# A copy of the SwiGLU gate by ScalarE between exponential and logarithm, in the filler of the recurrences

## The chip, the cores and the metric

The kernel runs on one core of one Trainium2 chip. The metric is the device time of the whole program in microseconds (us). The kernel before was timed three times on its own; beside these times there is one profiled execution, whose trace gives the start, the length and the waits of each instruction. TensorE is called PE in the rows, VectorE DVE, ScalarE ACT, GpSimd POOL, and SyncE, which issues the DMA transfers, SP.

## The reference, cut to what matters

The program is a trunk of two layers over one sequence of 1024 tokens with 1024 channels, all in fp32. Layer 0 mixes by forgetting attention and causal pooling, layer 1 by RWKV-7. Behind each mixer stands a SwiGLU feed-forward network (FFN) with 2816 inner columns, which are 22 blocks of 128:

```
def _swiglu(h, w_gate, w_up, w_down):
    return (jax.nn.silu(h @ w_gate) * (h @ w_up)) @ w_down

def _rwkv7_step(state, inp):
    r_t, w_t, k_t, v_t, a_t, b_t = inp
    sa = jnp.einsum('bhvk,bhk->bhv', state, a_t)
    state = (state * w_t[:, :, None, :] + sa[..., None] * b_t[:, :, None, :]
             + v_t[..., None] * k_t[:, :, None, :])
    return state, jnp.einsum('bhvk,bhk->bhv', state, r_t)
```

Here silu(z) is z times sigmoid(z). The change concerns how that product is formed in a part of the FFN blocks.

## The kernel before, in words

**Layout and products.** Channels lie on the 128 partitions, tokens on the free axis, in two halves of 512 tokens, so that the usual tile is 128x512. An fp32 matrix product is made from operands that are split into a high and a low part: `mm3` (lines 158 to 165) issues three matmuls for each block of 128 inner channels, L163 high by high, L164 with the low part of the activations, L165 with the low part of the weights. A weight block comes by `load_part`: a DMA into `wraw` (2 buffers), a cast on ACT to the high part (L151), a subtraction on DVE for the low part (L152).

**The two recurrences.** RWKV-7 is cut into four jobs: two groups of heads for half 0, then two for half 1. The function `job` first prepares its four pairs of heads (L1009 to L1091; L1032 and L1033 on ACT normalise kn, DVE's L1034 to L1044 make from it ZL and bk, and the matmuls L1060 take both). Then it solves triangular systems: DVE alone works through 30 steps of L1110 and L1112, turns the result with 32x32 transposes (L1120 into t, L1118 back into XR), and then PE multiplies (L1130), ACT and DVE copy the two halves of the result (L121 and L123, tile g), and PE multiplies again (L1140). Last comes the recurrence over eight chunks of 64 tokens, with matmuls that depend on each other (L1162 to L1191).

**The filler.** These jobs leave PE much free time, so FFN matmuls are woven in between. `job` and `ffn` are generators. `weave` asks the job for its next piece; the job says how many matmuls of filler shall stand there, and so many are then taken from the generator of the FFN. With jobs 1 and 2 it is the first FFN on half 1 (`f1`), with jobs 3 and 4 the second FFN on half 0 (`rest`). Job work runs in a stream of its own. On each engine the final order is made by a scheduler from the order of issue in the streams and from dependences; each engine then works through its list strictly in that order.

**A filler block.** For each block of 128 inner columns the gate projection fills a PSUM bank (24 matmuls), and ACT and DVE make silu from it (lines 713 to 726). Then, at every fourth block, comes the down projection of the previous group, `behind`: eight output blocks of 12 matmuls, each in a bank of its own, added into the residual x by DVE (L705). Then the up projection (24 matmuls), its multiplication with the gate (L732) and the split of the product for the next projection (L259 on ACT, L260 on DVE). All these blocks take their banks from a tag `fm` with two buffers (`using(..., mm=(pf, "fm", 2), ntbufs=3)`), in turn. A bank can be written again when its last reader has ended. The tile `sg` and, after the change, `gs` come from the tag "nt" with `ntbufs` = 3 buffers.

**The branch.** silu is made in three ways. Where the parameter `silu` is true, ACT has a function for it. Where `k.sigm` is true, ACT's sigmoid is used. In the recurrences' filler it is neither: there ACT keeps to exponential and logarithm, and L723 to L725 compute exp(-ln(1 + exp(-z))), which is sigmoid(z); L726 on DVE multiplies it with z, read from the bank. This last branch runs 42 times, between 1048 and 2320 us of the span.

Of the kernel before, what the change touches and what calls it, by code (L numbers as in the profile page):

```python
# [9 lines left out]
F32 = mybir.dt.float32  # L10
F32R = mybir.dt.float32r
AF = mybir.ActivationFunctionType
ALU = mybir.AluOpType
# [3 lines left out]
P = 128  # L17
# [3 lines left out]
HN = 512  # L21
# [92 lines left out]
def nm(k, s):  # L114
    k.uid += 1
    return f"{s}_{k.uid}"
# [9 lines left out]
def pmm(k):  # L126

    pool, tag, bufs = k.mm
    return pool.tile([P, HN], F32, tag=tag, name=nm(k, tag), bufs=bufs)
# [12 lines left out]
def load_part(k, ap, p, n, tag="w", w=512, bufs=None, pool=None):  # L142
    hi, lo = ((pool or k.wp).tile([P, w], F32R, tag=tag + i, name=nm(k, tag + i), bufs=bufs or k.wbufs) for i in ("hi", "lo"))
    raw = k.wp.tile([P, 512], F32, tag="wraw", name=nm(k, "wraw"), bufs=k.rawbufs)
    dst = raw[0:p, 0:n]
    if len(ap.shape) == 3:
        dst = dst.rearrange("p (a b) -> p a b", b=ap.shape[2])
    elif len(ap.shape) == 4:
        dst = dst.rearrange("p (a b c) -> p a b c", b=ap.shape[2], c=ap.shape[3])
    k.nc.sync.dma_start(dst, ap)  # L150
    k.nc.scalar.copy(hi[0:p, 0:n], raw[0:p, 0:n])  # L151
    k.nc.vector.tensor_tensor(lo[0:p, 0:n], raw[0:p, 0:n], rd(hi[0:p, 0:n]), ALU.subtract)  # L152
    return hi, lo


def mm3(k, out, pairs, first=True, last=True):

    nc = k.nc  # L160
    n = len(pairs)
    for i, ((wh, wl), (xh, xl)) in enumerate(pairs):
        nc.tensor.matmul(out, wh, xh, start=(first and i == 0), stop=False)  # L163
        nc.tensor.matmul(out, wh, xl, start=False, stop=False)  # L164
        nc.tensor.matmul(out, wl, xh, start=False, stop=(last and i == n - 1))  # L165
        yield 3
# [77 lines left out]
def blk(hl, j, w=P):  # L244
    c = j * w % 512
    hi, lo = hl[j * w // 512]
    return hi[:, c:c + w], lo[:, c:c + w]
# [435 lines left out]
def ffn(k, ins, L, halves, H, X, acc, tp, groups, after=None, silu=True, fb0=0):  # L683
    nc = k.nc

    def project(w):
        o = {half: pmm(k) for half in halves}
        for c in range(2):
            for half in halves:
                yield from mm3(k, o[half], [(blk(w, kt), H[half][kt]) for kt in range(4 * c, 4 * c + 4)], c == 0, c == 1)  # L690
        return o

    def down(n, fb0, acts, last):
        per = max(1, 4 // n)
        cur = None
        for half, m in [(half, m) for half in halves for m in range(8)] if last else [(half, m) for m in range(8) for half in halves]:
            if cur != m // per:
                cur = m // per
                w = []
                for f in range(0, n, 4):  # L700
                    c = min(4, n - f)
                    w.append(load_part(k, ins[f"wd{L}"][per * cur:per * cur + per, :, fb0 + f:fb0 + f + c].rearrange("m p f c -> p m f c"), P, per * c * P))
            o = pmm(k)
            yield from mm3(k, o, [(blk(w, (m % per) * n + i), acts[fb0 + i, half]) for i in range(n)])
            nc.vector.tensor_tensor(X[half][m], o, X[half][m], ALU.add)  # L705
            if last:
                after(half, m)


    behind = iter(())  # L710
    for gi, n in enumerate(groups):
        acts, sgs = {}, {}
        for fb in range(fb0, fb0 + n):
            g = yield from project(load_w(k, ins[f"wg{L}"][fb]))
            for half in halves:
                sg = sgs[half] = tp.tile([P, HN], F32, tag="nt", name=nm(k, "sg"), bufs=k.ntbufs)
                if silu:
                    k.last_silu = nc.scalar.activation(sg, g[half], AF.Silu)
                elif silu is None and k.sigm:
                    k.last_sig = nc.scalar.activation(sg, g[half], AF.Sigmoid)  # L720
                    nc.vector.tensor_tensor(sg, g[half], sg, ALU.mult)
                else:
                    nc.scalar.activation(sg, g[half], AF.Exp, scale=-1.0)  # L723
                    nc.scalar.activation(sg, sg, AF.Ln, bias=1.0)
                    nc.scalar.activation(sg, sg, AF.Exp, scale=-1.0)  # L725
                    nc.vector.tensor_tensor(sg, g[half], sg, ALU.mult)  # L726
            yield from behind
            behind = iter(())
            u = yield from project(load_w(k, ins[f"wu{L}"][fb]))
            for half in halves:  # L730
                sg = sgs[half]
                nc.vector.tensor_tensor(sg, u[half], sg, ALU.mult)  # L732
                acts[fb, half] = part(k, pair(k, *acc), sg)
        behind = down(n, fb0, acts, after and gi == len(groups) - 1)
        fb0 += n
    yield from behind
# [814 lines left out]
```

## Time and profile before

| what | value |
|---|---|
| three runs | 2705.3, 2699.98, 2703.82 us |
| median | 2703.82 us |
| profiled execution, its own time | 2699.79 us |
| span of its trace | 2698.0 us |
| TensorE busy | 2632.5 us, 98% of the span |
| VectorE busy | 1725.1 us, 64% |
| ScalarE busy | 1298.7 us, 48% |
| mean granted clock of TensorE | 0.996 of full speed |

The span is the stretch of the trace; the profiled execution's own time has the little that lies around it. Places in the program are given as microseconds from the span's start. Busy shares are averages over stages that differ: in the preparation and the solve of a job DVE is busy nearly all the time, in the recurrence over chunks PE is. A row of waits tells how long an engine stood still in all before the instructions of one line, and which engine, tile and line released it last. In a timeline the first number is the start, the second the length, and a bracket tells the idle time just before and its releaser. A matmul's length includes its passage through the array; successive matmuls overlap, so the time per matmul is read from successive starts.

### The profile page before, as it was taken

To read this page: it belongs to the slowest core of one execution; us is meant where nothing else is said; L and a number is where in the kernel's file an instruction comes from. 1 tells how busy PE (TensorE), PEld (TensorE's weight loads), DVE (VectorE), ACT (ScalarE), POOL (GpSimd) and SP (SyncE) were. 2 spreads that over 40 slices of the span, in tenths; PEclk is the share of its full clock that TensorE was granted. 3 is DMA by queue.
4 is the path that set the end of the run, shared out by engine and by line. 5 is a ranking of instruction groups with operands and counts; after the bars stand their busy time and mean duration, and the time that the engine had idled before them with its cause. 6 is when DMAs were issued, how large, how long until landed. Compare 5 with 4: busy or idle time off the path is not lost.

```text
span 2698.0 us, 40269 instructions
## 1 busy us (share of the span) xinstructions
PE 2632.5 (98%) x15368; PEld 2072.6 (77%) x15368; DVE 1725.1 (64%) x2940; ACT 1298.7 (48%) x2297; POOL 49.4 (2%) x139
## 2 busy tenths in 40 slices
PE   8999999999999999999999999999999999999999
PEld 6787878788888777777777677777777777888887
DVE  8777684653446655975995676469778856534443
ACT  7555564443224766434634467664445444332232
POOL 1000000000001000000000000000000000000000
PEclk9999999999999999999999999999999999999999
DMA  4111131233333545424433534554244336333333
GB/s 136 58 51 57 42 98 48 83 96 98 96 96 113 172 161 189 129 83 131 148 91 99 195 94 160 168 179 128 87 138 140 92 97 202 101 98 96 97 97 94
DMA packets 170529, 306.11 MB, mean 113 GB/s; under 512 B 18896, under 2 KB 26192, under 8 KB 170336
## 3 DMA queue, kind: packets, MB, share of 16 engines
q1 hardware_dynamic: 156512, 278.38, 33.5%
q10 hardware_dynamic: 13824, 25.17, 2.5%
q8 instruction: 120, 1.97, 0.3%
q14 instruction: 73, 0.60, 0.1%
HBM read 257.04 MB, written 46.43 MB: 112 GB/s over the span
## 4 chain that ended last, share of the span: by engine, by line
PE 77%; DVE 14%; ACT 3%; DMA 3%; issue 3%; SPq 0%; DVEq 0%; ACTq 0%
PE mm L163 16%; PE mm L164 16%; PE mm L165 16%; PE fm L163 6%; PE fm L164 5%; PE fm L165 5%; DVE wlo L152 2%; PE mm L175 1%; DVE nu L1112 1%; DVE pd L1110 1%; DVE ZL L1068 1%; DMA wraw<-in_wd_dram 1%; DMA wraw<-in_wu_dram 1%; ACT whi L151 1%; PE o L1177 1%
## 5 line engine op out<-in xcount | busy, mean ns | idle before, releaser
L151 ACT CAST whi<-wraw 128x512 fp32r<-128x512 f32 x738 | 454.0, 617 | 886.8 <-PE mm L164 484.5
L152 DVE TENSOR_TENSOR wlo<-wraw,whi 128x512 fp32r<-128x512 f32 x738 | 501.3, 683 | 446.0 <-ACT whi L151 436.4
L163 PE MATMUL mm<-hh,whi 128*128 128x512 f32 x864 | 343.7, 400 | 6.7 <-ACT hh L355 6.2
L165 PE MATMUL mm<-hh,wlo 128*128 128x512 f32 x864 | 338.7, 392 | 0.0
L164 PE MATMUL mm<-hl,whi 128*128 128x512 f32 x864 | 337.8, 392 | 0.0
L163 PE MATMUL mm<-uh,whi 128*128 128x512 f32 x728 | 283.5, 391 | 0.9 <-DVE x L1318 0.9
L165 PE MATMUL mm<-uh,wlo 128*128 128x512 f32 x728 | 283.1, 389 | 1.2 <-DVE wlo L152 1.2
L164 PE MATMUL mm<-ul,whi 128*128 128x512 f32 x728 | 283.2, 390 | 0.0
L163 PE MATMUL fm<-h1h,whi 128*128 128x512 f32 x528 | 218.7, 415 | 14.8 <-DVE sg L726 10.6
L165 PE MATMUL fm<-h1h,wlo 128*128 128x512 f32 x528 | 208.7, 396 | 0.5 <-DVE wlo L152 0.5
L164 PE MATMUL fm<-h1l,whi 128*128 128x512 f32 x528 | 208.5, 395 | 0.1
L163 PEld LDWEIGHTS mm<-hh,whi 128*128 128x128 f32 x864 | 162.5, 188 | 43.1 <-ACT hh L355 6.9
L165 PEld LDWEIGHTS mm<-hh,wlo 128*128 128x128 f32 x864 | 162.7, 188 | 34.8 <-DVE wlo L152 0.6
L164 PEld LDWEIGHTS mm<-hl,whi 128*128 128x128 f32 x864 | 162.9, 189 | 32.7 <-DVE hl L260 1.3
L163 PE MATMUL fm<-hh,whi 128*128 128x512 f32 x416 | 172.4, 414 | 3.5 <-ACT hh L259 2.8
L164 PE MATMUL fm<-hl,whi 128*128 128x512 f32 x416 | 164.5, 396 | 0.2 <-DVE hl L260 0.2
L165 PE MATMUL fm<-hh,wlo 128*128 128x512 f32 x416 | 164.6, 396 | 0.0
L163 PEld LDWEIGHTS mm<-uh,whi 128*128 128x128 f32 x728 | 136.5, 188 | 34.6 <-issue 2.7
L164 PEld LDWEIGHTS mm<-ul,whi 128*128 128x128 f32 x728 | 136.6, 188 | 31.1 <-issue 1.1
L165 PEld LDWEIGHTS mm<-uh,wlo 128*128 128x128 f32 x728 | 136.7, 188 | 30.0 <-DVE wlo L152 2.0
L705 DVE TENSOR_TENSOR x<-mm,x 128x512 f32<-128x512 f32 x96 | 66.2, 692 | 119.8 <-PE mm L165 119.6
L163 PEld LDWEIGHTS fm<-h1h,whi 128*128 128x128 f32 x528 | 99.5, 189 | 48.7 <-DVE sg L726 13.3
(338 smaller groups left out, 4632.4 us busy)
## 6 DMA issues: line engine op xcount, KB each, us to landing
wraw<-in_wg_dram SPq DMA_DIRECT2D x176, 256.0 KB, 2.8
wraw<-in_wu_dram SPq DMA_DIRECT2D x176, 256.0 KB, 2.7
wraw<-in_wd_dram SPq DMA_DIRECT2D x176, 256.0 KB, 2.7
wraw<-in_w_in_dram SPq DMA_DIRECT2D x52, 256.0 KB, 2.9
x<-in_xT_dram SPq DMA_DIRECT2D x32, 256.0 KB, 4.8
x<-x SPq DMA_DIRECT2D x32, 256.0 KB, 3.1
wraw<-in_w_k_dram SPq DMA_DIRECT2D x32, 256.0 KB, 2.9
wraw<-in_w_v_dram SPq DMA_DIRECT2D x32, 256.0 KB, 3.0
```

The costliest lines, as they stand in the source:

```text
L151: k.nc.scalar.copy(hi[0:p, 0:n], raw[0:p, 0:n])
L152: k.nc.vector.tensor_tensor(lo[0:p, 0:n], raw[0:p, 0:n], rd(hi[0:p, 0:n]), ALU.subtract)
L163: nc.tensor.matmul(out, wh, xh, start=(first and i == 0), stop=False)
L164: nc.tensor.matmul(out, wh, xl, start=False, stop=False)
L165: nc.tensor.matmul(out, wl, xh, start=False, stop=(last and i == n - 1))
L175: k.nc.tensor.matmul(out[n * q:n * q + n], w[:, n * j:n * j + n], xs[j], start=c == 0, stop=c + g == len(xs), tile_position=(0, n * q))
L705: nc.vector.tensor_tensor(X[half][m], o, X[half][m], ALU.add)
L1068: nc.vector.tensor_tensor(ZL[h][HS[1 - h], i, bs], s4[HS[1]], self.msk[HS[1]].rearrange("p a t -> p (a t)").unsqueeze(1).broadcast_to([64, ...
L1110: nc.vector.tensor_tensor(pv, nu[:, j + 1:32, j:j + 1].broadcast_to([P, n, j]), nu[:, j:j + 1, 0:j].broadcast_to([P, n, j]), ALU.mult)
L1112: nc.vector.tensor_tensor(nu[:, j + 1:32, 0:j], nu[:, j + 1:32, 0:j], pv, ALU.add)
L1177: nc.tensor.matmul(sp[HS[h], i], BK[h][:, i, c], uv[h][:, i], start=True, stop=True)
```

## The change

ScalarE copies the gate's bank into a new tile `gs` of 128x512 in SBUF, between the exponential and the logarithm. The multiplication on VectorE then reads this copy, no longer the bank. So the bank's last reader is the copy on ACT, no longer the multiplication on DVE. The other two ways to make silu stay as they are.

```diff
@@ -720,10 +720,13 @@
                     k.last_sig = nc.scalar.activation(sg, g[half], AF.Sigmoid)
                     nc.vector.tensor_tensor(sg, g[half], sg, ALU.mult)
                 else:
+
+                    gs = tp.tile([P, HN], F32, tag="nt", name=nm(k, "gs"), bufs=k.ntbufs)
                     nc.scalar.activation(sg, g[half], AF.Exp, scale=-1.0)
+                    nc.scalar.copy(gs, g[half])
                     nc.scalar.activation(sg, sg, AF.Ln, bias=1.0)
                     nc.scalar.activation(sg, sg, AF.Exp, scale=-1.0)
-                    nc.vector.tensor_tensor(sg, g[half], sg, ALU.mult)
+                    nc.vector.tensor_tensor(sg, gs, sg, ALU.mult)
             yield from behind
             behind = iter(())
             u = yield from project(load_w(k, ins[f"wu{L}"][fb]))
```

In the changed kernel every line from L726 on has a number that is 3 higher; the exponential is L725, the copy L726, the logarithm L727, the second exponential L728, and the multiplication L729. A number behind a tile's name counts tiles, so the same tile has another number in the changed kernel.

The first place is the solve of the first job, at 1161 us. This is ACT's list there before: two weight casts (whi), the three steps of a gate, two more casts, the split of the previous product (h1h), and ACT's half of the solve's g.

```order
L151 CAST whi_10637<-wraw_10639 128x512
L151 CAST whi_10744<-wraw_10746 128x512
L723 ACTIVATE sg_10574<-fm_10534 128x512
L724 ACTIVATE sg_10574<-sg_10574 128x512
L725 ACTIVATE sg_10574<-sg_10574 128x512
L151 CAST whi_10800<-wraw_10802 128x512
L151 CAST whi_10820<-wraw_10822 128x512
L259 CAST h1h_10627<-sg_10574 128x512
L121 COPY g_10683<-s_10650 32x512
```

And this is the same stretch of ACT's list in the changed kernel.

```order
L151 CAST whi_10649<-wraw_10651 128x512
L151 CAST whi_10758<-wraw_10760 128x512
L725 ACTIVATE sg_10584<-fm_10544 128x512
L726 COPY gs_10585<-fm_10544 128x512
L727 ACTIVATE sg_10584<-sg_10584 128x512
L728 ACTIVATE sg_10584<-sg_10584 128x512
L151 CAST whi_10814<-wraw_10816 128x512
L151 CAST whi_10834<-wraw_10836 128x512
L259 CAST h1h_10639<-sg_10584 128x512
L121 COPY g_10695<-s_10662 32x512
```

The copy stands directly behind its exponential; everything else keeps its sequence.

The second place is the end of the second job's solve, at 1389 us, on DVE: the transposes of the solve (into t and XR) between additions of filler blocks into the residual (x) and the low parts of weights (wlo). Before:

```order
L1120 STREAM_TRANSPOSE t_2906_13019<-nu_12626 128x32x32
L705 TENSOR_TENSOR x_4024<-fm_12951,x_4024 128x512
L1118 STREAM_TRANSPOSE XR_11847<-nu_12626 32x32x32
L705 TENSOR_TENSOR x_4130<-fm_12977,x_4130 128x512
L1118 STREAM_TRANSPOSE XR_11847<-nu_12626 32x32x32
L152 TENSOR_TENSOR wlo_13104<-wraw_13105,whi_13103 128x512
L152 TENSOR_TENSOR wlo_13159<-wraw_13160,whi_13158 128x512
L705 TENSOR_TENSOR x_4260<-fm_13006,x_4260 128x512
```

In the changed kernel:

```order
L1123 STREAM_TRANSPOSE t_2921_13049<-nu_12650 128x32x32
L705 TENSOR_TENSOR x_4024<-fm_12981,x_4024 128x512
L1121 STREAM_TRANSPOSE XR_11867<-nu_12650 32x32x32 x2
L705 TENSOR_TENSOR x_4130<-fm_13007,x_4130 128x512
L152 TENSOR_TENSOR wlo_13134<-wraw_13135,whi_13133 128x512
L152 TENSOR_TENSOR wlo_13189<-wraw_13190,whi_13188 128x512
L1121 STREAM_TRANSPOSE XR_11867<-nu_12650 32x32x32
L705 TENSOR_TENSOR x_4260<-fm_13036,x_4260 128x512
```

Both first transposes into XR now stand ahead of the addition into x_4130; before, one stood ahead of it and one behind.

The third place is the preparation of the fourth job, at 2046 us, on ACT: an exponential of the job (ep), then a gate's steps between those of the job's kn, and weight casts. Before:

```order
L1012 ACTIVATE ep_19768<-ld_19765 128x8x64
L723 ACTIVATE sg_19569<-fm_19490 128x512
L151 CAST whi_19708<-wraw_19710 128x512
L724 ACTIVATE sg_19569<-sg_19569 128x512
L1032 ACTIVATE kn_19565<-t_19567,eps 128x512
L725 ACTIVATE sg_19569<-sg_19569 128x512
L1033 ACTIVATE kn_19565<-kn_19565 128x512
L151 CAST whi_19749<-wraw_19751 128x512
```

In the changed kernel:

```order
L1015 ACTIVATE ep_19834<-ld_19831 128x8x64
L725 ACTIVATE sg_19633<-fm_19554 128x512
L726 COPY gs_19634<-fm_19554 128x512
L727 ACTIVATE sg_19633<-sg_19633 128x512
L1035 ACTIVATE kn_19629<-t_19631,eps 128x512
L728 ACTIVATE sg_19633<-sg_19633 128x512
L1036 ACTIVATE kn_19629<-kn_19629 128x512
L151 CAST whi_19774<-wraw_19776 128x512
L151 CAST whi_19815<-wraw_19817 128x512
```

The copy has the place of the weight cast, which moved behind the second step of kn.

## Rows read from the trace of the kernel before

**Rows 1.** The page's first part: busy time of each engine, share of the span, number of instructions.

```profile
PE 2632.5 (98%) x15368; PEld 2072.6 (77%) x15368; DVE 1725.1 (64%) x2940; ACT 1298.7 (48%) x2297; POOL 49.4 (2%) x139
```

**Rows 2.** What PE waited for in the whole span: us in total, number of waits, the longest.

```profile
PE fm L163 <- DVE sg L726: 14.0, 9, 4.1
...
PE s L1130 <- DVE t L1120: 4.2, 2, 2.3
```

**Rows 3.** Groups of instructions by line and form: busy us in total, mean ns of one, then the engine's idle time just before them with what ended it.

```profile
L796 ACT COPY ev<-mm 128x512 f32<-128x512 f32 x64 | 36.6, 583 | 33.7 <-PE mm L165 30.2 <-PE mm L884 1.9 <-ACT ev L796 0.8
...
L260 DVE TENSOR_TENSOR gl<-sg,gh 128x512 fp32r<-128x512 f32 x44 | 30.3, 689 | 6.5 <-ACT gh L259 4.3
L732 DVE TENSOR_TENSOR sg<-fm,sg 128x512 f32<-128x512 f32 x44 | 30.3, 688 | 29.0 <-PE fm L165 28.8
L726 DVE TENSOR_TENSOR sg<-fm,sg 128x512 f32<-128x512 f32 x42 | 28.9, 687 | 18.3 <-ACT sg L725 18.1
...
L724 ACT ACTIVATE sg<-sg 128x512 f32<-128x512 f32 x42 | 26.5, 631 | 1.0
...
L723 ACT ACTIVATE sg<-fm 128x512 f32<-128x512 f32 x42 | 24.9, 592 | 10.4 <-PE fm L165 10.3
```

**Rows 4.** Busy time in three stretches of preparation and solve (first, second and third job): the stretch and its length, then PE, PE's weight loads, DVE, ACT and POOL with their instructions, the granted clock of PE, the DMA share and GB/s.

```profile
1118.00:1160.00 42.00, 40.38 (x203) 32.51 (x202) 39.95 (x88) 20.21 (x36) 0.75 (x6) 1.00 0.35 107
...
1340.00:1400.00 60.00, 55.02 (x347) 44.36 (x348) 57.12 (x108) 24.26 (x45) 2.64 (x8) 0.97 0.32 97
1865.00:1900.00 35.00, 33.13 (x204) 26.84 (x203) 33.70 (x75) 10.45 (x18) 0.00 (x0) 1.00 0.28 84
```

**Rows 5.** The same view of 20 us in the recurrence over chunks (first job).

```profile
1200.00:1220.00 20.00, 20.00 (x243) 15.25 (x244) 10.85 (x21) 6.76 (x16) 0.00 (x0) 1.00 0.39 114
```

**Rows 6.** PE's timeline around the longest wait of rows 2: start, length, line, operation, output and inputs, and in brackets the idle time before it.

```profile
1163.73 0.39 PE L164 MATMUL fm<-h1l,whi 128*128 128x512 f32 x1
1163.96 0.39 PE L165 MATMUL fm<-h1h,wlo 128*128 128x512 f32 x1
1168.41 0.79 PE L163 MATMUL fm<-h1h,whi 128*128 128x512 f32 x1 [4.06 <-DVE sg L726]
...
1171.27 1.29 PE L1130 MATMUL s<-t,XR 32*32 32x32 f32 x64
1172.49 0.50 PE L163 MATMUL fm<-h1h,whi 128*128 128x512 f32 x1
...
1176.12 1.20 PE L1140 MATMUL s<-XR,g 32*32 32x32 f32 x64
```

**Rows 7.** ACT's timeline around the same place.

```profile
1160.88 0.62 ACT L151 CAST whi<-wraw 128x512 fp32r<-128x512 f32 x1 [3.09 <-DMA wraw<-in_wd_dram]
1161.40 0.59 ACT L723 ACTIVATE sg<-fm 128x512 f32<-128x512 f32 x1
...
1171.72 0.62 ACT L259 CAST h1h<-sg 128x512 fp32r<-128x512 f32 x1 [2.29 <-DVE sg L732]
1172.60 0.58 ACT L121 COPY g<-s 32x512 f32<-32x512 f32 x1 [0.27 <-PE s L1130]
```

**Rows 8.** DVE's timeline around the same place.

```profile
1160.67 4.04 DVE L1118 STREAM_TRANSPOSE XR<-nu 32x1024 f32<-32x1024 f32 x2
...
1171.00 0.68 DVE L732 TENSOR_TENSOR sg<-fm,sg 128x512 f32<-128x512 f32 x1
...
1173.21 0.70 DVE L123 COPY g<-s 32x512 f32<-32x512 f32 x1 [0.15 <-ACT g L121]
```

**Rows 9.** Timelines at the end of the second job's solve, of PE, then of ACT, then of DVE.

```profile
1385.93 0.50 PE L163 MATMUL fm<-h1h,whi 128*128 128x512 f32 x1 [2.79 <-DVE sg L726]
...
1386.90 0.63 PE L163 MATMUL fm<-h1h,whi 128*128 128x512 f32 x1
...
1389.46 0.63 PE L163 MATMUL fm<-h1h,whi 128*128 128x512 f32 x1
...
1382.31 0.59 ACT L723 ACTIVATE sg<-fm 128x512 f32<-128x512 f32 x1
...
1390.76 0.64 DVE L705 TENSOR_TENSOR x<-fm,x 128x512 f32<-128x512 f32 x1
1391.43 2.02 DVE L1118 STREAM_TRANSPOSE XR<-nu 32x1024 f32<-32x1024 f32 x1
```

**Rows 10.** Busy time, as in rows 4, of the eight microseconds around the wait of rows 6.

```profile
1164.00:1172.00 8.00, 3.94 (x48) 2.55 (x48) 7.91 (x9) 1.52 (x3) 0.00 (x0) 0.79 0.21 66
```

**Rows 11.** ACT's timeline in the preparation of the fourth job.

```profile
2046.43 0.58 ACT L723 ACTIVATE sg<-fm 128x512 f32<-128x512 f32 x1
2046.91 0.61 ACT L151 CAST whi<-wraw 128x512 fp32r<-128x512 f32 x1
```

**Rows 12.** Timelines around the same place, of PE, then of DVE.

```profile
2049.92 0.50 PE L163 MATMUL fm<-gh,whi 128*128 128x512 f32 x1 [2.71 <-DVE sg L726]
...
2054.68 1.49 PE L1060 MATMUL s<-ZL,bk 64*128 64x128 f32 x19
...
2053.79 0.68 DVE L1044 TENSOR_TENSOR bk<-ld,ld 128x512 f32<-128x512 f32 x1
```

**Rows 13.** What ACT waited for in the first two jobs (1040 to 1560 us), columns as in rows 2.

```profile
ACT uv L1173 <- PE s L1171: 20.0, 15, 3.1
```

**Rows 14.** What PE waited for at the end of the third job's solve (1885 to 1910 us).

```profile
PE s L1130 <- DVE t L1120: 1.9, 1, 1.9
```

## The prediction

> **What bounds the kernel now.** I read the totals first. TensorE (PE) is busy 2632.5 of 2698.0 us [rows 1], so all its idle time together is 65.5 us and no change to waits can give more. The list of what PE waited for comes next [rows 2]: its longest entry is the one this change aims at, 14.0 us in nine waits, where the first matmul of a new block (L163 into tile fm) waits for the multiplication L726. The reader is to see why: fm has two banks, and the gate keeps one of them until VectorE (DVE) has multiplied. Then come the prices of the five instructions concerned [rows 3], and last, for the stretches where these waits lie, the busy time of each engine [rows 4]. There the second fact shows. In the first stretch of a job (preparation, then the triangular solve) DVE is busy 39.95 of 42 us in the first, 57.12 of 60 in the second, 33.70 of 35 in the third: 95% and more. In the following stretch, the recurrence over chunks, PE is busy 20.00 of 20 us and the other two engines have slack [rows 5]. So a filler wait that goes in a solve stretch pays only as far as DVE lets PE run on.
>
> **The change, part by part.**
>
> *The added copies.* The branch runs 42 times. Each time ScalarE (ACT) reads 128x512 from PSUM once more. The trace has this operation elsewhere: L796, a COPY from a bank of the same shape, 583 ns [rows 3]. 42 x 0.583 = 24.5 us more on ACT, which is busy 1298.7 us [rows 1].
>
> *The multiplication* reads the copy instead of the bank. From PSUM L726 takes 687 ns; L260, the same kind of operation with both inputs in SBUF, 689 ns [rows 3]. No gain and no loss on DVE.
>
> The Trainium skill has a rule that speaks against the change here ("VectorE: DVE Perf Modes", Rules for kernel authors): for an elementwise operation on a matmul output, either take the single rate from PSUM or copy it out first if many operations follow. Here one follows. Rows 3 agree that the multiplication gains nothing; what the rule leaves out is the bank's release, and by the rule alone the sum would be a cost only.
>
> *The release of the bank.* Before, the bank is free after exponential, logarithm, exponential and multiplication: 0.592 + 2 x 0.631 + 0.687 = 2.54 us of work [rows 3], L725 taken like L724, plus queueing on two engines. After, it is free after 0.592 + 0.583 = 1.18 us, on one engine. In the new order 38 of the 42 copies stand directly behind their exponential, as at the first place shown with the change. So the wait on L726 itself should almost vanish, 14.0 us, plus what it does to the clock. Ordinarily two filler matmuls start 0.23 us apart (1163.73 and 1163.96 [rows 6]). After the wait of 4.06 us at 1164 the next six took from 1168.41 to 1171.27, 0.48 us each [rows 6]; the granted clock of that stretch is 0.79 [rows 10], so part of it ran at the lower level, 1.2 GHz. After the wait of 2.79 us at 1383 six starts lie between 1386.90 and 1389.46, 0.43 us apart, and eight matmuls ran so [rows 9]. Together 6 x 0.25 + 8 x 0.20 = 3.1 us. Full value of the waits: 17.1 us.
>
> What of it is kept I work out at the three waits over 2 us (9.6 of the 14.0 us).
>
> 1. At 1164 (solve of the first job). PE stops at 1163.96 + 0.39 = 1164.35 [rows 6]; the exponential ended at 1161.99 [rows 7], so with the copy the bank is free at about 1162.6 and PE runs on: six matmuls (1.4 us), L1130 (1.3 us; its inputs come from L1120 and the first two L1118, done by 1164.7 [rows 8]), and the filler that stands between L1130 and L1140, 1176.12 - 1172.49 = 3.6 us [rows 6]: to about 1170.5. Now it comes to L1140, which needs g. DVE's part of g (L123) stands behind L732 and ran at 1173.21, ACT's part (L121) at 1172.60 behind a cast that needs L732 [rows 7, 8]. The new order has the same sequence (first order shown), and DVE, busy 7.91 of 8 us there [rows 10], has no gap in which L732 could come earlier. L1140 can therefore start at 1173.9 to 1174.0 rather than 1176.12. **Gain 2.1 us**; PE now stands still for 3.5 us there, about as long as before, so I let the clock's loss stay. Bounds 0 and 4.06 + 1.5 = 5.6.
>
> 2. At 1383 (solve of the second job). The exponential ended at 1382.9, so the copy frees the bank at 1383.5, not 1385.9 [rows 9]. PE runs the second and third of the eight blocks of the down projection earlier, but the fourth needs the bank that L705 empties at 1390.76 + 0.64, behind a transpose [rows 9]: there 1.5 us of the start are left. In the changed order two transposes L1118 stand ahead of the next L705, on which the fifth block waits, where one stood (second order shown): 2.02 us more [rows 9], which takes those 1.5 us and half a microsecond besides, while the job gets its transposes earlier. **Gain 0.5 us**, bounds -1 (a loss) and 2.79 + 1.6 = 4.4.
>
> 3. At 2047 (preparation of the fourth job's second pair). The copy frees the bank at about 2047.6, so PE's wait, which ended at 2049.92, would be 2.3 us shorter [rows 11, 12]. But 4.8 us later PE comes to L1060, at 2054.68, and its input bk (L1044) was ready only at 2053.79 + 0.68 = 2054.47 [rows 12], at the end of a chain on DVE that begins with ACT's L1032 and L1033. The copy stands in ACT's queue ahead of both, in the place of a cast (0.61 us, begun 0.48 us behind the exponential [rows 11]) that now follows them (third order shown): the chain starts as before, and what PE wins at the bank it waits at L1060. **Nothing**, bounds 2.3 of gain and 3 of loss (the weight cast comes four places later, and its matmuls with it).
>
> The other six waits, 4.4 us together, lie in solve stretches with DVE at 95%: nought, bounds -4.4 and 0.
>
> *ACT's queue.* In the new order a job instruction is among the next three behind the copy at 20 of 42 places. If each were late by a whole copy and PE waited for it: 20 x 0.583 = 11.7 us. If ACT's slack covers them: 0. In the recurrences ACT stood idle 20.0 us in 15 waits before uv (L1173) in the first two jobs, 1.3 us each [rows 13], and PE never waits there [rows 5]. I take a value near that row: 1 us.
>
> The Trainium skill ("PSUM — Partial Sum Buffer", Engine vs sequencer instructions) calls the queues of ScalarE and VectorE strictly first in, first out. The trace shows it: the exponential of the first place started at 1161.40, right behind a cast that had waited 3.09 us for a transfer [rows 7]. By that rule a copy delays everything behind it unless a wait follows anyway; it gives the second rival its mechanism.
>
> *Moved work.* In the third job's solve L732 (0.688 us [rows 3]) now stands ahead of L1120, for which PE waited 1.9 us [rows 14]: cost 0.7 us, bounds 0 and 0.7. DMA issues on SP change place by one to three around the same stretches; weight loads keep their order, so I price them at nothing. The third buffer of tag nt now rotates over two tiles per block; the copy needs the sg of the block before, whose last reader L260 is done before the next gate's exponential: nothing.
>
> **Sum**: -2.1 - 0.5 + 0 + 1.0 + 0.7 = -0.9 us on the profiled execution's 2699.79 us, so 2698.9. The median of the runs is 2703.82, 4.0 us above that execution; on its scale **2703**.
>
> **Rivals.**
>
> *All of it is kept.* PE is the bound, DVE's last 5% and better order absorb the rest. For it: PE is busy 98%, its largest wait goes. Against: the points above, where the next wait is on DVE each time. On the median's scale 17.1 us less and 0 to 3 us of costs: 2687 to 2690; half of the gain, 2695 to 2697, counts here too.
>
> *ACT pays.* One mechanism: the copy sits between a gate's exponential and the job's own ACT work (kn, uv, XR copies), and the job's chain through DVE, which fills the preparation stretches to 95%, gets 0.58 us longer each time. It decides from the point where more than some 10 of the 20 places have no slack: 10 x 0.583 = 5.8 us, while the gains stay at 2.6. All 20 give +11.7 and, with moved work, 2699.8 + 11.7 + 0.7 - 2.6 = 2709.6, on the median's scale 2714. For it: in the third order shown the copy stands right ahead of kn's chain. Against: the slack of [rows 5, 13].
>
> *It doesn't do what it says*: the bank isn't free earlier because the exponential itself is late, blocked by a cast that waits for DVE or a transfer [rows 7]. Then the waits on L726 become waits on the copy, a little shorter; time as before, 2704.
>
> **How the numbers follow.** A change under 0.2%, 5.4 us, can't be told from none here. Chances: my forecast 0.42, the third rival 0.06 (both within 0.2%); all or half kept 0.28; ACT pays 0.24. Of the second half of each forecast's spread little crosses the line, so faster 0.29, same 0.48, slower 0.23. The range that holds 8 in 10 runs from the first rival's full gain to near the second's full price: 2688 to 2713. My forecast's own is 2698 to 2708.
>
> **What would show it.** The waits of PE on L726 gone and, in their place, waits of fm on L705 or of L1140 on L123 in the same solve stretches: right. PE's idle total near 65 us: right; near 48 us: first rival. PE waiting for L1171 to L1190's inputs or longer for bk and ZL, with ACT just before: second rival. A copy that takes over 0.6 us, or DVE's share in the solve stretches falling under 90%, would make my argument wrong.

## The result, and the profile after

The changed kernel took 2709.11 us (median of 13 runs, 2703.55 to 2712.55) against 2702.67 for the kernel before on the same chips: ratio 1.0022, 95% interval [1.0014, 1.0029]. That is 6 us slower (4 to 8), where 0.8 us less was forecast. The profiled execution took 2710.41 us, its span is 2708.6. This pair of traces lies further apart than the medians (2708.6 - 2698.0 = 10.6 us), so what is read from it below adds up to more than 6 us.

The page's first part for the changed kernel:

```profile
PE 2642.2 (98%) x15368; PEld 2081.5 (77%) x15368; DVE 1725.2 (64%) x2940; ACT 1314.1 (49%) x2339; POOL 51.8 (2%) x139
```

Against [rows 1] PE executes the same 15368 matmuls, but is busy 9.7 us longer. Its idle time is span less busy: 2708.6 - 2642.2 = 66.4 us, before 65.5. So in this trace the loss is not waiting. The same matmuls ran slower: the mean granted clock is 0.991, before 0.996. The 13 runs of the changed kernel point the same way: the two with a clock of 0.989 took 2711.2 us on average, the two with 0.994 took 2704.1.

What PE waited for in the changed kernel, whole span, columns as in [rows 2]:

```profile
PE fm L163 <- DVE x L705: 8.2, 6, 3.1
...
PE s L1063 <- DVE bk L1047: 6.1, 5, 2.4
...
PE s L1133 <- DVE t L1123: 5.9, 2, 3.4
PE s L1143 <- ACT g L121: 4.5, 1, 4.5
...
PE fm L163 <- DVE sg L735: 2.2, 1, 2.2
...
PE fm L163 <- ACT gs L726: 0.4, 1, 0.4
```

The 14.0 us before the multiplication are gone; 0.4 us are left before the copy. In their place stand other waits, several of them long: before the change the first five of these rows were 4.4, 4.4, 4.2, 0 and 0.2 us. The groups of the copy and of the multiplication answer to [rows 3]:

```profile
L729 DVE TENSOR_TENSOR sg<-gs,sg 128x512 f32<-128x512 f32 x42 | 28.9, 687 | 23.4 <-ACT sg L728 23.2
...
L726 ACT COPY gs<-fm 128x512 f32<-128x512 f32 x42 | 24.3, 579 | 0.1
```

Both cost what was forecast: 687 ns, and 579 where 583 was taken.

Where the time goes is read from landmarks: the first L1165 and the last L1171 of each job's recurrence, and L307, which begins the norm behind the first FFN. (They are named by the lines of the kernel before.) The changed kernel reaches the first job's recurrence 1.25 us earlier than before, the second's 3.23 us later, L307 10.05 us later, the third job's recurrence 11.03 and the fourth's 9.87 us later. Two stretches make the loss of this pair of traces: from the second job's preparation to its recurrence (4.5 us), and from the end of that recurrence to L307 (6.8 us). Busy time in these two, columns as in [rows 4], before:

```profile
1278.20:1419.40 141.20, 132.93 (x1017) 103.68 (x1015) 130.13 (x220) 69.89 (x125) 3.89 (x14) 0.99 0.40 124
1482.00:1549.80 67.80, 62.03 (x302) 44.31 (x301) 44.91 (x72) 30.06 (x53) 0.00 (x0) 1.00 0.57 192
```

and in the changed kernel:

```profile
1277.00:1422.60 145.60, 136.94 (x1017) 106.67 (x1015) 129.55 (x220) 71.41 (x130) 4.07 (x14) 0.95 0.39 119
1485.30:1559.90 74.60, 66.34 (x303) 47.48 (x302) 45.35 (x72) 31.05 (x55) 0.00 (x0) 0.93 0.53 174
```

In the first the number of matmuls is the same and PE's idle time nearly so (8.3 and 8.7 us); nearly all of the loss is clock, 0.95 instead of 0.99. In the second 2.5 of the 6.8 us are idle time (8.3 instead of 5.8), the rest is clock, 0.93 instead of 1.00.

A long wait and slow matmuls stand together in PE's timeline at the end of the second job's preparation. The kernel before, then the changed kernel:

```profile
1340.45 1.71 PE L1060 MATMUL s<-ZL,bk 64*128 64x128 f32 x21 [1.00 <-DVE bk L1044]
```

```profile
1343.11 2.21 PE L1063 MATMUL s<-ZL,bk 64*128 64x128 f32 x24 [2.36 <-DVE bk L1047]
1345.24 0.79 PE L165 MATMUL fm<-h1h,wlo 128*128 128x512 f32 x1
1345.83 0.63 PE L163 MATMUL fm<-h1h,whi 128*128 128x512 f32 x1
1346.26 0.63 PE L164 MATMUL fm<-h1l,whi 128*128 128x512 f32 x1
...
1354.54 0.63 PE L164 MATMUL fm<-h1l,whi 128*128 128x512 f32 x1
1354.96 0.46 PE L165 MATMUL fm<-h1h,wlo 128*128 128x512 f32 x1
```

After a wait of 2.36 us, which was 1.00 us before, filler matmuls start 0.43 us apart for ten microseconds; the granted clock there is 0.50, the level of 1.2 GHz. The Trainium skill ("TensorE: Matmul & The Clock Gate", HAM oscillation — how this bites in real kernels) warns that gaps in TensorE's work lower its clock in the middle of a kernel; this trace agrees at this place.

But the clock doesn't follow each time. The changed kernel was profiled once more (run `changed_again`, 2703.40 us). Its wait at this place is nearly as long:

```profile
1343.94 2.05 PE L1063 MATMUL s<-ZL,bk 64*128 64x128 f32 x24 [2.13 <-DVE bk L1047]
```

These are the same ten microseconds in the two traces of the changed kernel, first the one above, then this one, columns as in [rows 4]:

```profile
1345.00:1355.00 10.00, 10.00 (x42) 7.72 (x41) 8.28 (x12) 3.27 (x7) 1.89 (x2) 0.50 0.20 64
```

```profile
1345.00:1355.00 10.00, 10.00 (x92) 8.15 (x91) 9.58 (x12) 6.13 (x14) 1.89 (x2) 1.00 0.34 107
```

Against the kernel before, this second trace loses 1.7 and 2.6 us in the two stretches, where the first loses 4.5 and 6.8, and in the first stretch it loses by waiting (10.5 us of idle time instead of 8.3), not by clock. The main new waits are in both traces; what the clock adds to them differs from execution to execution.

At the end of the second job DVE's queue shows what moved. Before (the job's last outputs gn, and the additions of filler blocks into x):

```profile
1502.88 0.74 DVE L1218 SCALAR_TENSOR_TENSOR gn<-BK,cv,o 128x512 f32<-128x512 f32 x1
1503.54 0.69 DVE L1220 TENSOR_TENSOR gn<-gn,ld 128x512 f32<-128x512 f32 x1
1504.14 0.75 DVE L1219 SCALAR_TENSOR_TENSOR gn<-gn,cv,ld 128x512 f32<-128x512 f32 x1
1504.81 0.69 DVE L705 TENSOR_TENSOR x<-fm,x 128x512 f32<-128x512 f32 x1
1505.41 0.68 DVE L1220 TENSOR_TENSOR gn<-gn,ld 128x512 f32<-128x512 f32 x1
```

In the changed kernel:

```profile
1506.28 1.40 DVE L1221 SCALAR_TENSOR_TENSOR gn<-BK,cv,o 128x512 f32<-128x512 f32 x2
1507.60 1.41 DVE L1222 SCALAR_TENSOR_TENSOR gn<-gn,cv,ld 128x512 f32<-128x512 f32 x2
1508.92 1.28 DVE L1223 TENSOR_TENSOR gn<-gn,ld 128x512 f32<-128x512 f32 x2
1510.13 1.28 DVE L705 TENSOR_TENSOR x<-fm,x 128x512 f32<-128x512 f32 x2
```

The outputs are worked through in pairs now, and L705, which empties a filler bank, stands behind the last of them. PE waited for it 1.66 us before and 3.14 us after (the kernel before, then the changed one):

```profile
1505.64 0.47 PE L163 MATMUL fm<-h1h,whi 128*128 128x512 f32 x1 [1.66 <-DVE x L705]
```

```profile
1510.96 0.47 PE L163 MATMUL fm<-h1h,whi 128*128 128x512 f32 x1 [3.14 <-DVE x L705]
```

### The profile page after: what moved, and what is told of

Same layout as the page of the kernel before. It is cut to its first block, busy times and chain, and to the rows that moved or that the text cites. A ratio compares the mean times of both kernels' runs of the same rounds, so it can differ in the third digit from the quotient of the medians.

```text
span 2708.6 us, 40301 instructions
## 1 busy us (share of the span) xinstructions
PE 2642.2 (98%) x15368; PEld 2081.5 (77%) x15368; DVE 1725.2 (64%) x2940; ACT 1314.1 (49%) x2339; POOL 51.8 (2%) x139
## 4 chain that ended last, share of the span: by engine, by line
PE 77%; DVE 13%; DMA 4%; ACT 3%; issue 2%; SPq 0%; DVEq 0%; ACTq 0%
PE mm L163 16%; PE mm L164 16%; PE mm L165 16%; PE fm L163 6%; PE fm L165 5%; PE fm L164 5%; DVE wlo L152 2%; DVE nu L1115 1%; PE mm L175 1%; DVE pd L1113 1%; DMA y<-y 1%; DMA wraw<-in_wd_dram 1%; ACT whi L151 1%; PE o L1180 1%; PE s L1168 1%
## 5 line engine op out<-in xcount | busy, mean ns | idle before, releaser
L705 DVE TENSOR_TENSOR x<-mm,x 128x512 f32<-128x512 f32 x96 | 66.3, 692 | 118.5 <-PE mm L165 118.4
```

## The experiments

Three theories. **A**: the scheduler counts the full copies when it makes the order; the new order in a few places turns short waits of PE into long ones, and the lower clock behind them is the loss. **B**: the copies' own time, 24 us on ACT, delays the jobs (the second rival of the prediction). **C**: the earlier release lets PE run ahead into one long wait. Each version ran 5 to 12 times beside 22 to 35 runs of the kernel before on the same chip; the measured figure is the ratio of the two times with its 95% interval, and 0.001 of it is 2.7 us. Each version also has one trace. Single traces scatter: in the run with one copy at 1487 us the first job's recurrence comes 2.9 us later than before, with no copy yet made. So a landmark's shift of 2 or 3 us in one trace shows little; the length of a stretch between two landmarks scatters less.

**Copies without a use.** The edit of the tiny copy; the dead copy has its last line alone and keeps the full copy:

```diff
-                    nc.scalar.copy(gs, g[half])
+                    nc.scalar.copy(gs[:, 0:1], g[half][:, 0:1])
...
-                    nc.vector.tensor_tensor(sg, gs, sg, ALU.mult)
+                    nc.vector.tensor_tensor(sg, g[half], sg, ALU.mult)
```

> The copy takes one column instead of 512 and nothing reads it; VectorE multiplies from the bank as before the change. The scheduler's order is nearly that of before: 6 of 12962 matmuls, 14 of VectorE's and 2 of ScalarE's instructions stand elsewhere. Theory A (the loss comes from the order that the scheduler makes when it counts the full copies, through longer single waits and TensorE's lower clock behind them): the time of before, within 2 us. Theory B (the copies' own time on ScalarE delays the jobs): the same, within 2 us. Theory C (the bank's earlier release lets TensorE run ahead into one long wait): the same. A difference of more than 3 us would say that 42 more instructions cost by their number alone.

Measured: 0.9999 [0.9990, 1.0007]. 42 more instructions cost nothing by their number.

> The full copies are made, but VectorE multiplies from the bank as before, so the bank is not released earlier. The order is mostly that of the changed kernel: against it 89 matmuls stand elsewhere, against before 440. Theory A: 4 to 10 us above before, with the loss in the second job's preparation and in the stretch after its recurrence (1480 to 1550 us). Theory B: 6 to 12 us above before, since the copies' 24 us on ScalarE stay and all gains at the bank go. Theory C: within 2 us of before; the waits on the multiplication are back (14 us), and the mean granted clock is back at 0.996.

Measured: 1.0031 [1.0021, 1.0041], 8 us slower, in the ranges of A and B. PE waits for the multiplication again, nearly as before, and its idle time is 2708.9 - 2642.6 = 66.3 us, that of the two other kernels. Waits and PE's busy time of this run:

```profile
PE 2642.6 (98%) x15368; PEld 2081.8 (77%) x15368; DVE 1724.7 (64%) x2940; ACT 1318.4 (49%) x2339; POOL 51.3 (2%) x139
```

```profile
PE fm L163 <- DVE sg L729: 12.4, 7, 3.7
```

Without any release the loss is all there. Theory C falls.

**The copy behind the logarithm.**

```diff
-                    nc.scalar.copy(gs, g[half])
                     nc.scalar.activation(sg, sg, AF.Ln, bias=1.0)
+                    nc.scalar.copy(gs, g[half])
```

> The copy stands behind the logarithm instead of in front of it, so the bank is released some 0.6 us later than in the changed kernel; TensorE's order is the same as there, VectorE's the same but for 4 instructions. Theory A: the time of the changed kernel, 4 to 9 us above before. Theory B: the same, 4 to 9 us. Theory C: between before and the changed kernel, 3 to 6 us.

Measured: 1.0026 [1.0015, 1.0038], 7 us [4 to 10]. A and B both have it in their range, and C's upper part isn't excluded; this run tells nothing apart.

**The copy at a choice of places.** One edit serves for all; the gates are numbered 0 to 41 in the order of issue, 0 to 19 in the first two jobs.

```diff
+                    k.nsig = getattr(k, "nsig", -1) + 1
+                    on = k.nsig in {9, 10}
-                    gs = tp.tile([P, HN], F32, tag="nt", name=nm(k, "gs"), bufs=k.ntbufs)
+                    gs = tp.tile([P, HN], F32, tag="nt", name=nm(k, "gs"), bufs=k.ntbufs) if on else g[half]
...
-                    nc.scalar.copy(gs, g[half])
+                    _ = nc.scalar.copy(gs, g[half]) if on else None
```

The third and fourth job alone (20 to 41; here the condition was written `L == 1`):

> The copy is made only in the filler of the third and fourth job (22 of the 42 places); in the first two VectorE multiplies from the bank as before. TensorE's order there is that of before; in the last two jobs 47 matmuls stand elsewhere. Theory A: within 2 us of before, and probably 0 to 1 us under it, since the changed kernel's trace loses nothing in the last two jobs. Theory B: half of the loss, 3 to 4 us above before (22 of 42 copies). Theory C: 2 to 4 us above before, since the release is earlier at 22 places.

Measured: 1.0005 [0.9997, 1.0013]: 1 us [-1 to 4], where B wanted 3 to 4. It speaks for A; B's range is only just reached by the interval.

All of 0 to 19 but 0, 1, 9 and 10:

> The copy with the multiplication from it in 16 of the 20 places of the first two jobs: not in the four whose gate comes in a preparation (at 1048, 1060, 1271 and 1283 us), and not in the last two jobs. Against before 30 matmuls stand elsewhere. Theory A: within 2 us of before, or 1 to 2 us under it, since the waits at 1164 and 1383 go. Theory B: 16 of 20 places of a stretch that lost about 9 us: 5 to 7 us above before.

Measured: 1.0004 [0.9995, 1.0013], 1 us [-1 to 4], against B's 5 to 7. Its trace has a granted clock of 1.00 in the second job's preparation, but the wait of 3.1 us for L705, which ends at 1506 us, and it loses 3.3 us between the second job's recurrence and L307.

Only 0, 1, 9, 10, and only 9 and 10:

> The reverse: the copy only in the four places of the first two jobs' preparations. Against before 353 matmuls stand elsewhere, against the changed kernel 83. Theory A: 4 to 8 us above before with a tenth of the copies. Theory B: 4 copies by 0.58 us, so at most 2.3 us above before.

> The copy only in the two places of the second job's preparation (1271 and 1283 us). Against before 199 matmuls stand elsewhere, nearly all in that preparation. Theory A, narrowed to this place: 3 to 8 us above before. Theory B: two copies, at most 1.2 us above before.

Measured: 1.0009 [1.0000, 1.0017] and 1.0008 [0.9999, 1.0016], 2 us each: below A's ranges (from 4 and from 3 us) and at or above B's (up to 2.3 and 1.2 us), with intervals that reach into both. A missed here, and the time decides nothing. By the trace the wait for bk is 2.3 us with the two copies alone, and the granted clock behind it stays at 1.00:

```profile
PE s L1065 <- DVE bk L1049: 2.3, 1, 2.3
```

Only 5 and 14, the places of the two longest waits:

> The copy with the multiplication from it only at two places, those of the two longest waits (1161 and 1382 us). Every matmul stands where it stood before; 7 instructions of VectorE and 2 of ScalarE stand elsewhere. The prediction's points 1 and 2 give 2.1 + 0.5 = 2.6 us less; in the traces the first chunk of the first job should come about 2 us earlier and that of the second 2 to 3 us earlier. Theory A: 1 to 3 us under before. Theory B: the same less 1.2 us. Theory C (earlier release leads to one long wait): 0 to 2 us above before.

Measured: 0.9998 [0.9990, 1.0007]. Not told from before, and not from A's gain of 1 to 3 us either. In its trace the first job's recurrence comes 0.96 us earlier, of which 0.4 us were there before the first copy; the second's 0.93 us earlier. What each wait pays is less than single traces can show.

The solves alone (2 to 6, 11 to 14, 24 to 26, 33 to 36):

> The copy only in the 16 blocks of the four solve stretches. Against before 10 matmuls stand elsewhere. Theory A: 0 to 4 us under before, the gains without the new order; this is the candidate to beat both kernels. Theory B: 16 of 42 copies by 8 us, 2 to 3 us above before.

Measured: 1.0001 [0.9992, 1.0009]. Sixteen copies in nearly the order of before cost nothing that can be measured, and gain nothing.

All but 9 and 10:

> The copy at 40 of the 42 places: not at the two in the second job's preparation (1271 and 1283 us). The order of that preparation is that of before, everywhere else that of the changed kernel (231 matmuls stand elsewhere against before, 434 in the changed kernel). Theory A: 2 to 5 us less than the changed kernel, so 1 to 4 us above before; TensorE's wait for bk at the end of that preparation is back from 2.4 to 1.0 us. Theory B: 40 of 42 copies, 6 us above before.

Measured: 1.0014 [1.0006, 1.0023], 4 us [2 to 6], as A has it, with B's 6 us at the interval's end; the wait for bk is back at 1.0 us.

**ACT's time without the order.** The copy stands behind the multiplication and copies sg, in SBUF:

```diff
-                    nc.vector.tensor_tensor(sg, gs, sg, ALU.mult)
+                    nc.vector.tensor_tensor(sg, g[half], sg, ALU.mult)
+                    nc.scalar.copy(gs, sg)
```

with the copy between exponential and logarithm taken out. Nothing reads this copy.

> All 42 full copies are made by ScalarE, but behind the multiplication and of its product sg, in SBUF; nothing reads them, VectorE multiplies from the bank as before. The second job's preparation keeps before's order (against before 83 matmuls stand elsewhere, none between the first job's solve and the second job's recurrence). Theory A (order, and what follows from it in waits and clock): within 3 us of before. Theory B (24 us more on ScalarE delay the jobs): 5 to 9 us above before, as with the dead copies.

Measured: 1.0008 [1.0000, 1.0017], 2 us instead of the 8 of the dead copies, with the same 42 copies on ACT. In the two stretches of the loss its trace is 1.4 and 1.0 us later than before, that of the dead copies 5.5 and 3.1. In the second of them this run too has DVE's outputs in pairs and a wait of 3.2 us for L705, but the granted clock behind the wait is 1.00: here the turned order cost little.

The same with `g[half]` copied, so that the bank is held until the copy ends:

> All 42 full copies read the bank, but stand behind the multiplication, and nothing reads them; VectorE multiplies from the bank, which is so held 0.6 us longer than before the change. Against before 48 matmuls stand elsewhere, none of them in the first two jobs' preparations. Theory A (the order): 0 to 4 us above before; VectorE's and ScalarE's time is all there, the order is not. Theory B (24 us on ScalarE): 6 to 10 us above before, as the dead copies.

Measured: 1.0033 [1.0021, 1.0046], 9 us: theory A missed, and B's 6 to 10 us came out. The two stretches behave as A says (1.4 us later, 0.3 us earlier), but the trace loses 5.2 us between the third job's recurrence and the fourth's. PE now waits for the copy itself, 15.4 us over the span and 4.5 us in that stretch:

```profile
PE fm L163 <- ACT gs L729: 15.4, 8, 3.7
```

So a bank held longer may be a cost of its own; this run doesn't separate it from the copies' time, nor order from time.

Dead copies of half the width:

```diff
-                    nc.scalar.copy(gs, g[half])
+                    nc.scalar.copy(gs[:, 0:256], g[half][:, 0:256])
```

> The dead copies in half width: 256 of 512 columns are copied, nothing reads them, VectorE multiplies from the bank. TensorE's order in the second job's preparation is word for word that of the dead copies (394 matmuls stand elsewhere against before). Theory A: 5 to 9 us above before, about as the dead copies. Theory B: half of the time on ScalarE, 3 to 5 us above before.

Measured: 1.0021 [1.0012, 1.0029], 6 us [3 to 8]: in A's range of 5 to 9, but the interval holds B's 3 to 5 too. The trace says more: the order of the second job's preparation is that of the dead copies, ACT's time is half, and the stretch loses 5.2 us where the dead copies lost 5.5. Neither has a long wait for bk at the end of it; both have one of 1.2 to 1.3 us for ZL earlier on, and the lower clock behind that one (granted 0.63 from 1320 to 1334 us with the dead copies, 1.00 in the kernel before).

**One copy**, at gate 18, 1487 us:

> One single copy, with the multiplication from it, at the gate of 1487 us behind the second job's recurrence. 18 matmuls and 38 of VectorE's instructions stand elsewhere, all there. Theory A: TensorE's wait for the addition L705 at about 1505 us rises from 1.7 to 3.1 us, as in the changed kernel; 0 to 3 us above before. Theory B: 0.6 us of ScalarE at one place: that wait stays at 1.7 us, the time is that of before.

Measured: 1.0016 [1.0007, 1.0025], 4 us [2 to 7] from a single instruction of 0.58 us. That is above A's 0 to 3, whose upper part the interval covers, and B's nothing is excluded. DVE's outputs go in pairs as in the changed kernel, and the wait is there. PE's waits from 1482 to 1562 us, of this run:

```profile
PE fm L163 <- DVE x L705: 3.5, 2, 3.2
```

and of the kernel before:

```profile
PE fm L163 <- DVE x L705: 2.0, 2, 1.7
```

Its trace lies 2.9 us behind before's at the first job's recurrence and still 2.9 us at the end of the second's, so nothing is lost up to the copy; from there to L307 it loses 3.4 us. This is theory A by itself; B has nothing to put in its place.

The changed kernel again, beside it:

> The changed kernel once more, on the same chip as the three others. 4 to 9 us above before by every theory; TensorE's idle time near 66 us and the mean granted clock 0.989 to 0.994.

Measured: 1.0032 [1.0020, 1.0044]. Its trace, shown with the result, has a mean granted clock of 0.994 and 66.9 us of idle time.

**The reverse.** All copies but gate 18, and all but 9, 10 and 18:

> The copy at 41 of the 42 places: not at 1487 us. VectorE's order behind the second job's recurrence is that of before but for 2 instructions, elsewhere that of the changed kernel. Theory A: the wait for L705 at about 1505 us is back at 1.7 us, and the time is 3 to 4 us less than the changed kernel's, 2 to 4 us above before. Theory B: 41 of 42 copies, the changed kernel's time, 6 to 8 us above before.

> The copy at 39 of the 42 places: not at 1271, 1283 and 1487 us. Theory A: within 2 us of before. Theory B: 39 of 42 copies, 5 to 8 us above before.

Measured: 1.0010 [1.0000, 1.0020] and 0.9995 [0.9987, 1.0004]. With 39 of the 42 copies the kernel is at before's time (2701.22 against 2703.56 us). B wanted 6 to 8 and 5 to 8 us. Three places hold the whole loss; B is out as a cost of each copy. The waits of that last run in the second job, 1275 to 1425 us:

```profile
PE fm L163 <- ACT gs L728: 2.3, 1, 2.3
...
PE s L1065 <- DVE bk L1049: 1.0, 1, 1.0
```

**All traces beside one another.** The two stretches tell the versions apart more sharply than the times do. From the end of the first job's recurrence to the second's, the nine traces whose full or half copies stand at gates 9 and 10 ahead of the last exponential are 1.7 to 8.2 us longer than before; the ten others lie between 0.7 us shorter and 1.4 longer. From the second recurrence to L307, the ten traces with DVE's outputs in pairs all have a wait of 3.1 to 3.2 us for L705 and are 1.0 to 6.8 us longer; the nine others have a wait of 1.3 to 1.7 us and are 0.3 to 0.9 us shorter. The clock follows the waits often, not always: behind the wait of 3.1 to 3.2 us it fell in eight of ten traces, behind the shorter one in none of ten, before's trace included; behind a wait of over 2 us for bk it fell in four of six, behind one of 1.0 us in none of eleven. What no version has is the new order without any copy; at gates 9 and 10 the order is told from ACT's time only by the half copies.

**VectorE relieved.**

```diff
-                    nc.vector.tensor_tensor(sg, gs, sg, ALU.mult)
+                    nc.gpsimd.tensor_tensor(sg, gs, sg, ALU.mult)
```

> As the changed kernel, but GpSimd multiplies the copy with the gate instead of VectorE; this takes 28.9 us off VectorE, mostly in stretches where it is 95% busy. Against the changed kernel 154 matmuls stand elsewhere. Theory A: the order of the second job's preparation is a new one, so the loss stays or halves: 0 to 8 us above before, and if VectorE's load was the cause, under before. Theory B: as the changed kernel, 6 us above before, since ScalarE has the same copies.

Measured: 1.0064 [1.0050, 1.0078], 17 us slower. One multiplication takes 1364 ns there:

```profile
L729 POOL TENSOR_TENSOR sg<-gs,sg 128x512 f32<-128x512 f32 x42 | 57.3, 1364 | 752.0 <-ACT sg L728 690.2 <-DVE S L1187 52.2 <-DVE wlo L152 9.6
```

That is twice DVE's 687, as the Trainium skill has it ("GPSIMD Engine Reference", Engine selection). PE's idle time rises to 2721.6 - 2647.8 = 73.8 us. DVE was hardly relieved by it: with 42 instructions fewer it is busy 1722.5 us, against 1725.2 in the changed kernel. Most instructions of DVE that begin while GpSimd multiplies end only behind that multiplication (31 of 36). This one took 1.31 us; in the changed kernel its like takes 0.33:

```profile
1132.43 1.35 POOL L729 TENSOR_TENSOR sg<-gs,sg 128x512 f32<-128x512 f32 x1 [3.78 <-ACT sg L728]
1132.66 1.31 DVE L1115 TENSOR_TENSOR nu<-nu,pd 128x168 f32<-128x168 f32 x1
```

So this run doesn't test what DVE's load is worth.

No version beat both kernels clearly; the 39 copies come nearest.

## Why the prediction was wrong, point by point

**Right.** The copy's price (579 ns), the multiplication's (687 ns), the end of the waits on L726, and PE's idle time, forecast near 65 us and measured 66.4. Point 1 came nearly as worked out: PE ran on and then waited for g, 4.5 us instead of the 3.5 forecast. DVE was 1.1 us early when it came to this place (its transpose into t started at 1157.35, before at 1158.43), and L1143 got its g at 1172.75, where the working gives 1173.9 - 1.1. But in this trace the step "I let the clock's loss stay" failed: the wait was followed by more slow matmuls than before (L1143 itself took 1.91 us instead of 1.20), and little of the 2.1 us was left: from the transpose to the first L1165 the changed kernel took 0.2 us less than before (1189.81 - 1157.35 against 1191.06 - 1158.43), the run with two copies 0.6 us less. Over all traces but GpSimd's this stretch takes 32.1 to 33.2 us (mean 32.7) with a copy there that the multiplication reads and 32.6 to 35.4 (mean 33.7) without: a gain nearer to 1 us than to 2.1, with ranges that overlap. Point 2: 0.5 forecast, too small for these runs to show. Point 3: nothing forecast; between the third and fourth job's recurrences this trace gains 1.2 us, but kernels without a copy in these jobs lie there between 1.0 us shorter and 0.2 longer, so that is within the scatter.

**Wrong: the step "Moved work".** It priced one place, L732 ahead of L1120, at 0.7 us, and rightly (PE's wait there rose from 1.87 to 2.54 us); the rest of the new order it took for nothing. Two other places decided. At the end of the second job's recurrence, where a single copy turns DVE's order, the price is 4 us [2 to 7]; in the second job's preparation, two copies, 2 us [0 to 4]. Together they are the 6 us. At neither place did PE wait for L726, so the sum had no term for either. The prediction put the six small waits all into solve stretches; one of them, 0.43 us at 1533 us, lies behind the second job's recurrence, in the very stretch where most was lost.

**Wrong: the price of a wait.** The sum counted waits by their length, and the clock only as a gain, 3.1 us, at waits that go. The idle time was forecast rightly, yet the time wasn't: in the first pair of traces PE was busy 9.7 us longer with the same matmuls, most of it at the lower clock behind waits that were new or longer. In the second trace of the changed kernel it was 2.2 us longer, beside 1.4 us more of idle time.

**"ACT's queue", 1.0 us, and the second rival.** The sign was the rival's, the mechanism wasn't. 39 copies at 0.58 us cost nothing that can be measured, their gains included. The rule that the prediction cites at the multiplication from the Trainium skill ("VectorE: DVE Perf Modes", Rules for kernel authors), to copy out of PSUM only where many operations follow, speaks against the change; the sign of all 42 copies agrees, 39 of them cost nothing that can be measured.

**The first rival** (all of it kept) fell: the waits moved, as forecast. **The third** (the bank isn't free earlier) fell too: of 14.0 us of waits 0.4 are left.

**Open.** Which waits the clock follows. In one trace of the changed kernel the wait of 2.36 us for bk was followed by ten slow microseconds, in the other the same wait, 2.13 us long, by none; before, one of 2.71 us at 2047 was followed by none either ([rows 12]). In the 13 runs 0.001 of mean clock goes with about 1.5 us; why a kernel's runs differ among themselves by 9 us is not shown. Open too is why the turned order cost 4 us with one copy at 1487 us and only 1 or 2 us, with intervals down to nothing, where 15 other copies or the copies in SBUF stood beside it.

## What to carry to other kernels

Where a scheduler makes the order, an edit's price is the order that comes out, not only the instructions that went in: compare the orders over the whole program, and look at every place that moved, above all at DVE instructions that empty a bank, not only at the waits aimed at. When TensorE is 98% busy, read idle time and granted clock apart: a wait moved from several places into one long one costs nothing in the sum of waits and can still cost time, in some executions and not in others. So take a second trace before you explain one. To find the place, put the edit at a few of its sites and then at all but those.

## What the runs showed of the hardware that was not expected

One copy of 0.58 us on ACT changed a program of 2700 us by 4 us [2 to 7]. Runs of one and the same kernel differ by 9 us (2703.55 to 2712.55), and go roughly with the mean granted clock (0.989 to 0.994). The same wait of the same program was followed by a granted clock of 0.50 in one execution and of 1.00 in another. With 42 multiplications moved to GpSimd DVE was busy only 2.7 us less, not 28.9. In the twenty profiled executions but GpSimd's, PE's idle time lies between 62 and 68 us, while its busy time for the same 15368 matmuls goes from 2630 to 2647 us.
